# Block products in the linear memory's output projection, and a residual kept off chip

## The chip, the cores and the metric

One core of a Trainium2 chip runs one inference step of a hybrid encoder layer. A core has a matrix engine (TensorE, PE in the profile, with PEld for its weight loads), three engines for elementwise work (VectorE = DVE, ScalarE = ACT, GpSimd = POOL), and SyncE (SP), which here only issues DMAs. Matmuls read operands from the on-chip memory and accumulate in banks of a small second memory (PSUM); DVE and ACT read the banks. The metric is the device time of one execution in microseconds.

## The reference

The layer takes 512 frames of a new stream and 64 of a running one, 576 columns in all, 1024 features wide.

```python
h = layer_norm(ALPHA * x + 0.5 * swiglu_ffn(x, ffn1_w_gu, ffn1_w_down), ln1_g, ln1_b)
z = h @ w_in                       # mLSTM q,k,v,o,i,f | attention q,k,v | gates g_ml, g_att
h_ml  = mlstm(conv(q), conv(k), v, i, f)          # 4 heads of 256, matrix memory, chunks of 64
h_ml  = norm_per_head(h_ml) * ml_norm_g * sigmoid(o)
y_ml  = h_ml @ w_ml_proj                          # 1024 x 1024
y_att = band_attention(...) @ w_att_proj          # 1024 x 1024
merged = sigmoid(g_ml) * y_ml + sigmoid(g_att) * y_att
h = layer_norm(ALPHA * h + merged @ w_out, ln2_g, ln2_b)
y = layer_norm(ALPHA * h + 0.5 * swiglu_ffn(h, ffn2_w_gu, ffn2_w_down), ln3_g, ln3_b)
```

Beside y the step returns the attention's keys and values, the convolution's history and the memory's state. All of it is fp32. The change lies in `y_ml`, `merged` and the residual `ALPHA * h`.

## The kernel before

**Data.** Activations lie transposed: a tile has 128 features in its partitions and 576 columns (time), and 1024 features are eight tiles. A weight tile has 128 partitions and 1024 numbers: the eight 128x128 blocks of one output tile.

**fp32 out of two parts.** A matmul takes rounded operands. Each operand is split into a high part (ACT rounds it) and a low part (the difference, by DVE's tensor_tensor at L150), and each product is three matmuls: high x high, high x low, low x high. For weights in the list `ADDED` the low part is made another way (`add_lo`): ACT writes minus the high part, and a DMA issued by POOL (L197) adds the original to it in place.

**A plain gemm** (`gemm`) computes an output tile as 8 blocks x 3 matmuls in two halves of the columns, 256 and 320: 48 matmuls.

**Block products** (`seven`). Two output tiles j, j+1 and the two halves of the columns (A = 288 to 576, B = 0 to 288) and of the features form a 2x2 block product, which is computed with seven block products instead of eight, in Winograd's form: 7 products x 4 blocks x 3 = 84 matmuls of 288 columns. They need sums of weight blocks and of activation blocks, and sums of results. `seven` takes the weight operands by the names a, u, t, b: a = the first tile's weights, b = half of the second's, u and t = sums (`split_ds`, two raw tiles; t's sums are the last readers of a's raw tile). The order is X from a; Y from a; X += t; Z from u; X += u; Z (or Y) += t; X += b, and after each product `step(n)` runs: ACT copies X after the first and third product, and Z after the fourth, DVE does the rest. X is copied while its bank goes on accumulating, so the next product into X has to wait for the copy. The feed-forward layers and, in four pairs, the attention's projection (`ap_pair`) are computed this way before the change.

**Weights** come through four split buffers (`NWB = 4`) and two raw buffers, in the order of the list `plan`. `pump` loads ahead and splits the next weight when a buffer is free; `done` frees a buffer after its last product.

**Order.** PE's instructions run in the order in which they are written. A small planner (`Order`, `later(dt, fn)`) counts PE time and writes delayed work between the matmuls. The other engines' instructions are ordered by the compiler, by priority (`tc.high_priority(offset=...)`) and readiness; on the chip each engine then works in its fixed order. `issue_after` puts one instruction behind another.

**The stage that changes.** The four heads of the matrix memory run one after the other; a head's last work are transposes (L143) of `hf`, after which two tiles `og` with the head's output are appended to `HF`. Under the last head three gate tiles (60, 61, 62) are computed. After the last head: `gate(7)`, one more gate tile, under which `ht_split` splits the eight tiles HF; then eight plain gemms ("mp", j) with the matmul operand H; each result half is multiplied by its gate on DVE, the attention's part (`matt`, loaded from DRAM tile MD by SP) is added by POOL, and the sum is split into `mg`, the operand of the out projection ("o", j).

**The residual.** The operands H of w_in (the first norm's output in two parts, 16 of the 24 buffers of the pool `slots`) stay on chip until the second norm takes both parts as its residual (two DVE operations per half tile, `Norm.residual`). The second norm's own result goes to DRAM (XD) for the third norm, which loads it again; the `mg` tiles have a pool of their own.

Of the kernel before, what the change touches and what calls it, by code (L numbers as in the profile page):

```python
# [10 lines left out]
F32 = mybir.dt.float32  # L11
# [6 lines left out]
P = 128  # L18
NP_ = 512
NS = 64  # L20
# [66 lines left out]
def tile_layer(ctx: ExitStack, tc: tile.TileContext, ins, outs):  # L87
# [75 lines left out]
    def blank(out, like, behind=None):  # L163
# [15 lines left out]
        | {("ap", j) for j in range(KT)} | {("gu2", 1, 1)}  # L179
# [27 lines left out]
    ds = {}  # L207

    def split_ds(c):
# [8 lines left out]
        def put(a, t):  # L218
            n = t.shape[1]
            ds["hi"] = act(hi[:, a:a + n], t)  # L220
            tt(lo[:, a:a + n], t, f(hi[:, a:a + n]), ALU.subtract)
# [3 lines left out]
        elif what == "u":  # L225
            own = plan[c][0][0] == "dsap" and plan[c][0][1] > 0
            room = lambda: (slot(F32, opool[0], "o") if own else slot(F32))[:, :512]
# [110 lines left out]
    def gemm(tiles, xs, cbs, passes=NORMAL, tags=None):  # L338
# [7 lines left out]
        for p, (tl, hl) in enumerate(passes):  # L346
            nch = len(tiles[tl[0]])
            k0 = 0
            for c in range(nch):
# [4 lines left out]
                for i in range(nk):  # L354
                    k = k0 + i
                    ww = slice(i * P, (i + 1) * P)
                    st, sp = k == 0, c == nch - 1 and i == nk - 1
# [92 lines left out]
    plan += [(("mp", j), ins["w_mp"][j]) for j in range(KT)]  # L450
# [85 lines left out]
    class Norm:  # L536
        def __init__(self, xs, scale, eps, gi, final=None, keep=False, away=None):
            self.away = away
# [37 lines left out]
        def collect(self, j, hf, ps):  # L576
# [11 lines left out]
            else:  # L588
# [6 lines left out]
                if j < KT - 1 and (self.away is None or j + 1 not in DS):  # L595
                    self.residual(j + 1, hf)
# [20 lines left out]
        def shift(self, hf, dh):  # L617
# [3 lines left out]
            dr = self.lp.tile([P, 320], F32R, tag="dr", name=nm("dr"))[:, :n] if self.away is None else \  # L621
# [9 lines left out]
            if self.away is not None and hf == 1:  # L631
# [3 lines left out]
        def moments(self, j, hf, dh):  # L635
# [9 lines left out]
            if j == KT - 1 and self.away is not None:  # L645
                wst["behind"] = last
            if j == KT - 1:
                later(L_JOINT if hf and self.away is not None else L_STATS, lambda: self.stats(hf))
# [8 lines left out]
        def stats(self, hf):  # L657
# [16 lines left out]
            later(J_SPREAD if hf and self.away is not None else L_SPREAD, lambda: self.spread(hf, dg))  # L674
# [61 lines left out]
        def apply(self, j, hf, rb):  # L736
# [9 lines left out]
            if self.final is None:  # L746
# [91 lines left out]
    def seven(name, j, blocks, X, Y, Z, step):  # L838
# [16 lines left out]
        own = name == "dsap"  # L855
# [300 lines left out]
    XD = [away("xd") for _ in range(KT)]  # L1156

    def ffn(xs, n, gi, raw, final=None, prev=None):
        hh = {}
        with tc.tile_pool(name=nm("hr"), bufs=FT, side="right", reuse_waits="tile") as hr, \  # L1160
# [92 lines left out]
            with tc.tile_pool(name=nm("h1"), bufs=n1, side="right", reuse_waits="tile") as h1, \  # L1253
# [4 lines left out]
                          away=[ins["xT"][:, k] for k in range(KT)] if prev is None else XD)  # L1258
# [582 lines left out]
    sgp = gstack.enter_context(tc.tile_pool(name="sg0", bufs=4, side="right", reuse_waits="tile"))  # L1841
# [4 lines left out]
    mp = mstack.enter_context(tc.tile_pool(name="ml", bufs=1, reuse_waits="tile"))  # L1846
# [450 lines left out]
```

## Time and profile before

| | us |
|---|---|
| runs shown: lowest, median, highest of 3 | 1547.39, 1547.59, 1549.40 |
| span of the profiled execution | 1546.8 |
| PE busy | 1531.3 (99%) |
| DVE busy | 1160.4 (75%) |
| ACT busy | 882.5 (57%) |
| POOL busy | 196.6 (13%) |
| last transposes of the last head | 1034.25 |
| eight plain gemms of the linear memory's projection | 1041.74 to 1092.52 |
| second feed-forward layer begins | 1145.17 |

The profile's own execution is told by its span, from the first to the last instruction; what lies around it isn't listed apart. Times are in microseconds from the span's start. In a timeline row stand start, duration, engine, line, operation, output <- inputs, shape and count, and in brackets how long the engine stood before it and what released it; matmuls overlap, so the distance of their starts is what one costs. A row of groups has busy time and mean ns behind the first bar. A windows row has, for each engine, the busy time in that stretch and the count of instructions, then PE's granted clock, DMA's busy share and GB/s. Names such as s, o, H, wh, wl are the program's tiles: wh and wl the high and low part of a weight, wr its raw tile, s a buffer of `slots`, os and H the split operands of the attention's and the linear memory's projection, mg that of the out projection.

### The profile page before, as it was taken

Reading aid. Unit: us, or ns where it says so; the run is one execution under the profiler, and the core shown is the slowest. Engines: PE = TensorE matmul, PEld = TensorE weight load, DVE = VectorE, ACT = ScalarE, POOL = GpSimd, SP = SyncE. Lnnn points to the kernel's source line nnn. Section 1 sums busy time; section 2 is a strip of 40 time slices with the busy share of each in tenths; the row PEclk is TensorE's granted clock in tenths of the full one; section 3 lists DMA queues with packets and bytes.
Section 4 is the critical chain, followed back from the end, with each engine's and each line's share of the span. In section 5 each row is a group of like instructions: output and inputs, shape, how many; then the busy total and the mean of one; then the engine's idle time right before and its main releaser. Section 6 shows DMA issues by size and latency. Waiting matters only on the chain.

```text
span 1546.8 us, 29458 instructions
## 1 busy us (share of the span) xinstructions
PE 1531.3 (99%) x11587; PEld 1516.3 (98%) x11587; DVE 1160.4 (75%) x2186; ACT 882.5 (57%) x1670; POOL 196.6 (13%) x370
## 2 busy tenths in 40 slices
PE   9999999999999999999999999999999999999997
PEld 9999999999999999999999999999999999999997
DVE  7877778756899767887677577775688787787756
ACT  7545446533766557777864877753456454557323
POOL 1000000100200015545200321102120000001000
PEclk9999999999999999999999999999999999999999
DMA  8322223535544449687544965542653223217244
GB/s 246 109 101 91 93 99 102 130 108 146 172 152 143 156 167 239 153 209 169 139 107 147 283 148 133 130 132 82 199 126 104 108 82 110 82 69 190 78 128 150
DMA packets 82228, 213.18 MB, mean 138 GB/s; under 512 B 9513, under 2 KB 23209, under 8 KB 82089
## 3 DMA queue, kind: packets, MB, share of 16 engines
q1 hardware_dynamic: 66088, 172.29, 33.8%
q0 software_dynamic: 14848, 37.30, 13.7%
q8 instruction: 91, 1.49, 0.4%
q10 hardware_dynamic: 1152, 1.70, 0.3%
q14 instruction: 49, 0.39, 0.1%
HBM read 174.82 MB, written 22.22 MB: 127 GB/s over the span
## 4 chain that ended last, share of the span: by engine, by line
PE 84%; DVE 7%; ACT 3%; DMA 3%; issue 2%; POOL 1%; SPq 0%; ACTq 0%; DVEq 0%; POOLq 0%
PE mm L133 69%; PE aux L133 14%; PE aux L143 2%; DVE wl L150 1%; DVE sc L1537 1%; DVE s L150 1%; DVE s L153 1%; ACT wh L147 1%; ACT sc L147 1%; DMA s<-in_xT 1%; DVE o L150 1%; DVE kl L150 1%; DVE sc L157 1%; DMA wr<-in_w_ap 0%; DMA kh<-kh 0%
## 5 line engine op out<-in xcount | busy, mean ns | idle before, releaser
L133 PE MATMUL mm<-s,wh 128*128 128x288 f32 (+2 forms) x3430 | 700.8, 298 | 0.7 <-DVE s L150 0.2
L133 PEld LDWEIGHTS mm<-s,wh 128*128 128x128 f32 x3430 | 548.3, 189 | 3.8 <-DVE s L150 1.6
L133 PE MATMUL mm<-s,wl 128*128 128x288 f32 (+2 forms) x1705 | 503.3, 295 | 0.0
L133 PEld LDWEIGHTS mm<-s,wl 128*128 128x128 f32 x1705 | 321.1, 188 | 0.2 <-DVE wl L150 0.2
L147 ACT ACTIVATE wh<-wr 128x1024 fp32r<-128x1024 f32 (+2 forms) x136 | 133.0, 979 | 141.0 <-PE mm L133 81.7
L133 PE MATMUL mm<-tx,wh 128*128 128x288 f32 x778 | 158.4, 296 | 0.0
L150 DVE TENSOR_TENSOR wl<-wr,wh 128x1024 fp32r<-128x1024 f32 (+2 forms) x97 | 108.9, 1126 | 57.1 <-ACT wh L147 57.0
L133 PEld LDWEIGHTS mm<-tx,wh 128*128 128x128 f32 x778 | 124.9, 188 | 0.0
L133 PE MATMUL mm<-tx,wl 128*128 128x288 f32 x383 | 113.0, 295 | 0.6 <-DVE wl L150 0.6
L925 ACT ACTIVATE wh<-wt 128x1024 fp32r<-128x1024 f32 x53 | 56.2, 1060 | 88.4 <-DVE wt L150 88.4
L150 DVE TENSOR_TENSOR wl<-wt,wh 128x1024 fp32r<-128x1024 f32 x53 | 64.7, 1222 | 52.3 <-ACT wh L925 51.0
L133 PE MATMUL mm<-h,wh 128*128 128x256 f32 (+2 forms) x384 | 78.3, 295 | 0.0
L150 DVE TENSOR_TENSOR wl<-wu,wh 128x1024 fp32r<-128x1024 f32 x50 | 61.2, 1224 | 21.6 <-ACT wh L925 21.6
L197 POOL DMA_DIRECT2D s<-s x16 | 13.7, 854 | 495.0 <-ACT s L147 252.8
L133 PEld LDWEIGHTS mm<-tx,wl 128*128 128x128 f32 x383 | 72.0, 188 | 0.9 <-DVE wl L150 0.9
L147 ACT ACTIVATE h<-h 128x288 f32<-128x288 f32 x80 | 34.9, 437 | 65.2 <-DVE h L150 65.1
L925 ACT ACTIVATE wh<-wu 128x1024 fp32r<-128x1024 f32 x50 | 52.9, 1058 | 32.7 <-PE mm L133 32.5
L150 DVE TENSOR_TENSOR wl<-ws,wh 128x1024 fp32r<-128x1024 f32 x53 | 64.6, 1219 | 0.1
L150 DVE TENSOR_TENSOR ws<-wu 128x1024 f32<-128x1024 f32 x53 | 64.5, 1217 | 0.0
L133 PEld LDWEIGHTS mm<-h,wh 128*128 128x128 f32 x384 | 61.5, 188 | 0.2
L925 ACT ACTIVATE ah<-wu 128x512 fp32r<-128x512 f32 x53 | 33.4, 631 | 44.8 <-PE mm L133 41.3
L133 PE MATMUL mm<-h,wl 128*128 128x256 f32 (+2 forms) x192 | 56.5, 294 | 0.0
(399 smaller groups left out, 3612.6 us busy)
## 6 DMA issues: line engine op xcount, KB each, us to landing
wu<-in_w_gu SPq DMA_DIRECT2D x80, 512.0 KB, 4.3
wr<-in_w_in SPq DMA_DIRECT2D x46, 512.0 KB, 3.7
wr<-in_w_dn SPq DMA_DIRECT2D x40, 512.0 KB, 3.6
wl<-in_w_in POOLq DMA_DIRECT2D x38, 512.0 KB, 6.8
wu<-in_w_in SPq DMA_DIRECT2D x26, 512.0 KB, 4.5
wr<-in_w_dn SPq DMA_DIRECT2D x20, 384.0 KB, 3.7
s<-s POOLq DMA_DIRECT2D x16, 288.0 KB, 3.7
wr<-in_w_ap SPq DMA_DIRECT2D x8, 512.0 KB, 3.6
```

Source lines behind the costliest of these rows:

```text
L133: PE.matmul(out, lhsT, rhs, start=start, stop=stop, **kw)
L143: PE.transpose(out, in_, idn)
L147: return ACT.activation(out, in_, func, **kw)
L150: return (eng or DVE).tensor_tensor(out, a, b, op=op)
L153: return DVE.scalar_tensor_tensor(out=out, in0=a, scalar=s, in1=b, op0=op0, op1=op1)
L157: return (eng or DVE).tensor_scalar(out=out, in0=a, scalar1=s1, scalar2=s2, op0=op0, **kw)
L197: return POOL.dma_start(lo, src, accum_op=ALU.add)
L925: self.last = ACT.activation(hi, src, AF.Copy)
L1537: DVE.tensor_tensor_reduce(out=out, in0=ps, in1=g, op0=ALU.add, op1=ALU.min, scale=-1.0, scalar=3e38, accum_out=acc)
```

## The change

The linear memory's projection keeps its first two output tiles as plain gemms; the other six become three pairs of block products ("dsmp"). For that:

- the rows of w_ml_proj are reordered on the host so that blocks i and 4 + i of the product are HF[2i] and HF[2i+1], and the plain gemms take their blocks in the order 0, 4, 1, 5, ...;
- `whole(i)` splits two tiles of HF as before, and `blocks(i)` makes the sums of halves in place (four half-width DVE operations), rounds two sums and makes two low parts, most of them with `add_lo`. `first_blocks` does this for HF[0] to HF[3] and one block pair under the end of the last head, at low priority; a pool `mq` now holds what the heads no longer need by then and is closed for it;
- the weights a and b of a pair, and the two plain tiles' weights, get their low part by `add_lo` (ACT copy and POOL DMA); the sums u and t have four buffers of their own (`qpool`);
- the attention's part is added for six of eight tiles by an accumulating DMA of POOL from DRAM into the gated tile, which is split 10500 planner units later; the last pair adds two loaded tiles on DVE and splits in parts;
- `mg` lies in `slots`, in buffers that H leaves;
- the first norm's result is written to DRAM (XH, 16 stores on SP), and the second norm loads its residual from there (eight loads on SP, behind the last weight load), one DVE operation per half tile.

```diff
+    qpool = []
...
             ds["hi"] = act(hi[:, a:a + n], t)
+            if plan[c][0][0] == "dsmp" and what in "ab":
+                add_lo(lo[:, :n], hi[:, :n], plan[c][1])
+                return
             tt(lo[:, a:a + n], t, f(hi[:, a:a + n]), ALU.subtract)
...
-    plan += [(("mp", j), ins["w_mp"][j]) for j in range(KT)]
+    plan += [(("mp", j), ins["w_mp"][j]) for j in range(2)]
+    for j in range(2, KT, 2):
+        a, b = ins["w_mp"][j], ins["w_mp"][j + 1]
+        plan += [(("dsmp", j, x), w) for x, w in (("a", a), ("u", b), ("t", None), ("b", b[:, :512]))]
...
                     act(dh, dh, AF.Identity, bias=b_)
-                    if self.away is None:
-                        SP.dma_start(XD[j][:, t0:t0 + n], dh)
+                    SP.dma_start(self.store[j][:, t0:t0 + n], dh)
...
             tt(Wl[:w, :n], d[:w, :n], f(Wh[:w, :n]), ALU.subtract)
+            if h == 3 and b == 4:
+                later(0, first_blocks)
...
+    def whole(i):
+
+        r = HF[2 * i], HF[2 * i + 1]
+        for e in range(2):
+            hi, lo = HT.p[4 * e + i] = slot(F32R, htp[i > 1], "H"), slot(F32R, htp[i > 1], "H")
+            act(hi, r[e])
+            tt(lo, r[e], f(hi), ALU.subtract)
+
+    def blocks(i):
+
+        r2, r1 = HF[2 * i], HF[2 * i + 1]
+        (h2, l2), (h1, l1) = HT.p[i], HT.p[4 + i]
+        hp_, lp_, hm, lm = (slot(F32R, htp[i > 1], "H") for _ in range(4))
+        tt(r1[:, A], r1[:, A], r1[:, B], ALU.subtract)
+        tt(r1[:, B], r2[:, B], r1[:, B], ALU.subtract)
+        stt(r2[:, B], r1[:, A], -1.0, r2[:, B], ALU.mult, ALU.subtract)
+        stt(r2[:, A], r2[:, B], -1.0, r2[:, A], ALU.mult, ALU.subtract)
+        for hi, lo, r in ((hp_, lp_, r2), (hm, lm, r1)):
+            wst["rounded"] = act(hi, r)
+            if i < 2 or r is r1:
+                add_lo(lo, hi, r)
+            else:
+                tt(lo, r, f(hi), ALU.subtract)
...
+    def first_blocks():
+        bstack.close()
+        htp.append(hts.enter_context(tc.tile_pool(name="ht0", bufs=16, side="right", reuse_waits="tile")))
+        with tc.high_priority(offset=-1500):
+            for i in range(2):
+                whole(i)
+            blocks(0)
...
-    od.bg.append((1300, ht_split()))
-    matt = [slot(F32) if j < 4 else slot(F32, gmp, "gm") for j in range(KT)]
-    for m, d in zip(matt, MD):
-        SP.dma_start(m, d)
+    with tc.high_priority(offset=300):
+        for i in range(2, 4):
+            whole(i)
+    for i in range(1, 4):
+        blocks(i)
+    matt = {j: slot(F32) for j in (KT - 2, KT - 1)}
+    for j, m in matt.items():
+        SP.dma_start(m, MD[j])
...
+    def mp_pair(j):
+        X, Y, Z = bank("mm")[:, :HT_], bank("aux")[:, :HT_], bank("mm")[:, :HT_]
...
+            if last:
+                e, cc = {5: (1, B), 6: (0, slice(0, T)), 7: (1, A)}.get(n, (0, None))
+                if cc is not None:
+                    with tc.high_priority(offset=60 if n == 7 else 0):
+                        tt(sg[j + e][:, cc], sg[j + e][:, cc], matt[j + e][:, cc], ALU.add)
+                        split(e, cc)
+            elif n > 5:
+                POOL.dma_start(sg[j + n - 6], MD[j + n - 6], accum_op=ALU.add)
+                later(10500, lambda: split(n - 6))
...
+        seven("dsmp", j, HB, X, Y, Z, step)
...
-    for j in range(KT):
-        gemm(one(("mp", j)), HT, [mp_cb(j)])
+    for j in range(2):
+        gemm(one(("mp", j)), HT, [mp_cb(j)], order=(0, 4, 1, 5, 2, 6, 3, 7))
+    for j in range(2, KT, 2):
+        mp_pair(j)
+    od.drain()
...
-    ln2 = Norm(H, ALPHA, EPS, 1, keep=True)
+    ln2 = Norm(H, ALPHA, EPS, 1, keep=True, away=XH, store=XD)
+    with tc.issue_after(wst["load"].ins):
+        for j in range(KT):
+            ln2.fetch(j, SP)
```

More of the change, by code (lines that the diff above doesn't have):

```diff
@@ L336, in get, with gemm @@
             return self.p[k]
-    def gemm(tiles, xs, cbs, passes=NORMAL, tags=None):
+    def gemm(tiles, xs, cbs, passes=NORMAL, tags=None, order=None):
         ids = {}
@@ L594, in collect @@
                     self.moments(j, hf, dh)
[L595 removed]
+                if j < KT - 1 and not (self.down and j + 1 in DS):
                     self.residual(j + 1, hf)
@@ L630, in shift @@
             self.shifted.add(hf)
-            if self.away is not None and hf == 1:
+            if self.down and hf == 1:
                 for j in range(2, LAST[1]):
```

135 lines of the change are left out of this document (80 added, 55 removed).

## The prediction

> **What bounds the kernel now.** I read the page first, then the waits of PE, then the windows of the stages around the linear memory's projection, then PE's timeline of that projection and of the attention projection, which already runs as block products.
>
> ```profile
> span 1546.8 us, 29458 instructions
> PE 1531.3 (99%) x11587; PEld 1516.3 (98%) x11587; DVE 1160.4 (75%) x2186; ACT 882.5 (57%) x1670; POOL 196.6 (13%) x370
> PE aux L143 <- DVE ptl L150: 2.1, 4, 1.0
> PE mm L133 <- ACT o L147: 0.2, 1, 0.2
> ```
>
> ```profile
> core 0: us, PE busy (x) PEld busy (x) DVE busy (x) ACT busy (x) POOL busy (x), PEclk, DMA share, GB/s
> 790.00:803.00 13.00, 13.00 (x100) 13.00 (x99) 13.00 (x27) 8.36 (x16) 0.00 (x0) 1.00 0.13 42
> 1042.00:1054.00 12.00, 12.00 (x94) 12.00 (x92) 6.81 (x11) 4.27 (x7) 2.35 (x3) 1.00 0.29 87
> 1054.00:1066.00 12.00, 12.00 (x94) 12.00 (x93) 6.45 (x10) 3.90 (x6) 3.23 (x4) 1.00 0.22 77
> 1105.00:1118.00 13.00, 13.00 (x101) 13.00 (x100) 11.25 (x27) 6.42 (x9) 0.84 (x1) 1.00 0.78 187
> ```
>
> PE is busy for 99% of the span, at clock 1.00, and its longest wait is 1.0 us. So only two things move the time: matmul work taken away, and new waits of PE. In the projection (1042 to 1092) DVE is a little over half busy and ACT a third: that is the room into which the change puts its additions.
>
> The profiled execution has a span of 1546.8; the median shown is 1547.59, 0.8 above it. The sum is made on the span, and 0.8 is added at the end. I call a change within 0.2% (3.1 us) no change, about what a measurement of this kernel can tell.
>
> **The change part by part. PE.**
>
> ```profile
> 1041.74 0.40 PE L133 MATMUL mm<-H,wh 128*128 128x256 f32 x2
> 1048.09 0.40 PE L133 MATMUL mm<-H,wh 128*128 128x256 f32 x2
> 803.55 0.43 PE L133 MATMUL mm<-os,wh 128*128 128x288 f32 x2
> 814.67 0.42 PE L133 MATMUL mm<-os,wh 128*128 128x288 f32 x2
> 840.84 0.53 PE L133 MATMUL mm<-os,wh 128*128 128x288 f32 x2 [0.23 <-ACT o L147]
> 849.07 0.40 PE L133 MATMUL mm<-s,wh 128*128 128x256 f32 x2
> ```
>
> A plain tile takes 1048.09 - 1041.74 = 6.35, a pair 12.70 (96 matmuls). The first pair of the attention projection, 84 matmuls of 288 columns, takes 814.67 - 803.55 = 11.12. Three pairs save 3 x 1.58 = 4.74: the most that the change can bring. The attention projection's four pairs took 849.07 - 803.55 = 45.52, 11.38 each, because its third products had to wait (the row at 840.84 is one). At that mean three pairs save 3 x 1.32 = 3.96. I take 3.96, since the new pairs have the same order of products and copies.
>
> [...]
>
> **Operands of the projection.** Before: eight splits of HF, then nothing. After: the same eight, plus 16 half-width sums on DVE, eight roundings on ACT, and eight low parts: two on DVE, six as an ACT copy and an accumulating DMA of POOL.
>
> ```profile
> 1031.97 1.69 DVE L157 TENSOR_SCALAR hf<-hf,mv,mrs 128x256 f32<-128x256 f32 x5
> 1034.25 1.25 PE L143 MATMUL aux<-ident,hf 128*128 128x128 f32 x10
> L150 DVE TENSOR_TENSOR H<-og,H 128x576 fp32r<-128x576 f32 x8 | 5.7, 755 | 0.4 <-ACT H L147 0.3
> L147 ACT ACTIVATE H<-og 128x576 fp32r<-128x576 f32 x8 | 5.0, 675 | 0.0
> L147 ACT ACTIVATE wh<-wr 128x1024 fp32r<-128x1024 f32 x10 | 10.6, 1059 | 15.8 <-PE mm L133 15.8
> 806.98 0.45 DVE L150 TENSOR_TENSOR o<-o,aux 128x288 f32<-128x288 f32 x1 [1.90 <-PE aux L133]
> 817.41 0.69 DVE L150 TENSOR_TENSOR wl<-o,wh 128x512 fp32r<-128x512 f32 x1 [0.23 <-ACT wh L147]
> 828.10 0.63 ACT L147 ACTIVATE wh<-o 128x512 fp32r<-128x512 f32 x1 [3.02 <-DVE o L150]
> 828.63 0.39 ACT L147 ACTIVATE o<-mm 128x288 f32<-128x288 f32 x1
> ```
>
> HF0 to HF3 and the first block sums fit the holes under the last head. What remains must be done between the end of the last transposes (1034.25 + 1.25 = 1035.5) and the first product that takes a block sum, third in its pair, at 1041.74 + 12.70 + 2/7 x 11.12 = 1057.6: 22.1 us. ACT then has 4 splits and 10 block operations (14 x 0.675), four weight passes (4 x 1.06), the half passes of u and t (4 x 0.63) and three gate copies (0.4 each): 17.4. DVE has 4 x 0.755, 12 x 0.45, 2 x 0.755, u and t 8 x 0.69, four gatings and four og products (0.45 each): 19.0. Side by side both fit under the last gate's matmuls and the plain pair; before the attention projection DVE was full for 13 us (first windows row) and PE stayed busy. Cost 0; if that cover fails because the two wait for each other in turn, the price is that of a rival below.
>
> **Weights.** Per pair before: 2 x 1.06 on ACT and two low parts on DVE. After: a and b low parts by ACT copy and POOL DMA, u and t sums on DVE: ACT 2.12 + 4 x 0.63 + 1.26 = 5.9, DVE 8 x 0.69 = 5.5. With evictions (ACT 3 x 0.4, DVE 5 x 0.45 + 0.755) and the splits of two result tiles (ACT 1.35, DVE 1.5) a pair has 8.5 us of ACT and 10.0 of DVE in 11.12. DVE at 90% is what makes waits likely. The rows at 828 show how: ACT stood 3.02 us at a weight rounding that wanted a DVE sum, and the copy of X queued behind it ran at 828.63, so the next product into X started late. The 11.38 contains two such waits.
>
> New against that pattern is the low part of a:
>
> ```profile
> 806.78 1.06 ACT L147 ACTIVATE wh<-wr 128x1024 fp32r<-128x1024 f32 x1 [0.97 <-PE aux L133]
> 980.39 1.06 ACT L147 ACTIVATE wh<-wr 128x1024 fp32r<-128x1024 f32 x1 [0.56 <-PE mm L133]
> 981.72 1.06 ACT L147 ACTIVATE wl<-wh 128x1024 fp32r<-128x1024 f32 x1
> 983.08 0.85 POOL L197 DMA_DIRECT2D wl<-in_w_in  x1 [0.99 <-ACT wl L147]
> L197 POOL DMA_DIRECT2D wl<-in_w_in x18: 844/860/952, 852.3 to 1008.4; - x18
> DMA to landing us min/median/max: 5.3/6.1/11.0
> ```
>
> With four weight buffers the next a can be rounded only when this pair's a is free, 806.78 - 803.55 = 3.23 after the pair's start. From rounding to DMA issue is 983.08 - 980.39 = 2.69, landing 5.3 at best and 6.1 at the median of the 18 in 840 to 1015. That is 11.2 to 12.0 after the start, and PE wants it with the next pair's third matmul, two matmuls of 11.12 / 84 = 0.13 in: at 11.39. Behind the DMA's wait for the copy POOL has only the DMAs that add the attention part, which have a pair's time. So at two pair starts the wait is 0 to 0.6, and ACT's queue can add 0.5. As a late start also gives the third product time, it partly replaces the wait counted in the 11.38. I take 0.1 each, 0.2; ends 0 and 2.2.
>
> ```profile
> 828.77 2.61 SPq L266 DMA_DIRECT2D wr<-in_w_ap  x2
> 832.29 1.06 ACT L147 ACTIVATE wh<-wr 128x1024 fp32r<-128x1024 f32 x1 [0.74 <-DMA wr<-in_w_ap]
> ```
>
> There the next a was even loaded late (its raw buffer waits for the t sums), 832.29 being 6.5 after that pair's start (814.67 + 11.12). With own buffers for the sums the new t sums can run earlier; if not, the last pair's a lands 3 us later. That is in the upper end.
>
> **Around it.** Last pair to out projection: after the sixth product come an eviction, a gating, an addition, a rounding and a low part, 0.45 + 2 x 0.755 + 0.675 + 0.755 = 3.4 and hops; the last product (11.12 / 7 = 1.6) and the six steps before k = 6 (6 x 0.35, from 6.35 by columns) give 3.7. I take 0.2; ends 0 and 1.5, as DVE is busy. hf is ready at 1033.66, 0.59 before the transposes; one low-priority split of 0.755 in front of it costs 0.2, so 0.1 (ends 0 and 0.6). The other parts:
>
> ```profile
> 1098.42 0.28 PE L133 MATMUL aux<-dr,ones_r 128*128 128x256 f32 x1
> s<-xd SPq DMA_DIRECT2D x6, 288.0 KB, 4.9
> s<-s POOLq DMA_DIRECT2D x16, 288.0 KB, 3.7
> 401.48 0.36 SPq L266 DMA_DIRECT2D wr<-in_w_in  x1
> 415.15 0.65 SPq L1687 DMA_DIRECT2D s<-in_vpast  x1
> 1141.22 0.46 PE L133 MATMUL aux<-mg,wh 128*128 128x320 f32 x2
> 1144.35 0.40 ACT L147 ACTIVATE s<-s 128x256 fp32r<-128x256 f32 x1
> 1145.17 0.50 PE L133 MATMUL mm<-s,eh 128*128 128x256 f32 x2
> ```
>
> Adding the attention part by accumulating DMA (3.7 to land) takes 16 POOL additions away and has a pair's time; nothing waits. The residual from memory: eight loads of 288 KB queue on SP behind the out weights. The first, issued about when the out projection starts and landing in 4.9, then passes one DVE and one ACT operation before the mean matmul, which stands 5.9 after that start (1098.42 - 1041.74 - 8 x 6.35): 0, ends 0 and 0.5. It also takes one of two DVE operations of each residual away, 16 x 0.45 = 7 us in a stage where DVE is 11.25 of 13 busy; PE does not wait there, so 0. The 16 new stores after the first norm, about 0.36 us each on SP, should mostly fall into SP's hole from 401.84 to 415.15, with no weight load queued behind them: 0, ends 0 and 0.5. At the second norm the new operands take over buffers of the out projection's input; PE's last pass frees the first two within 0.5 us of 1141.22, two more each 0.44 us, and ACT first writes at 1144.35, so that still fits.
>
> Sum: 1546.8 - 3.96 + 0.2 + 0.2 + 0.1 = 1543.3; with 0.8, 1544.1.
>
> **The rivals.** *Waits eat half.* Pair starts 2.2, third products as before (0.78 for three pairs at the mean), edge 1.0, tail and first residual 0.6: 4.6 of waits, 1546.8 - 4.74 + 4.6 + 0.8 = 1547.5; over a whole band of 1.7 to 7.8 us of waits the time is within 0.2%, middle 1546. For it: DVE at 90%, tight landings. Against: the same structure lost 1.0 in four pairs. 0.30.
>
> *The first block pair starts late: slower.* Place: the 22.1 us computed above. ACT's 17.4 and DVE's 19.0 feed each other, each in its written order; without any overlap they need 36.4, 14.3 too long, and the time is 1546.8 - 4.74 + 14.3 + 0.8 = 1557. For it: ACT's 3.02 us stand at 828.10 is such a wait. Against: the full DVE of 790 to 803. It decides for slower where less than 6.5 us of ACT's work overlaps (a wait of 7.8); 0.12, at about 1552 in the middle.
>
> *The accumulating DMAs land late: slower.* Two pair starts wait L - 5.4 each; at L = 9.5 that is 8.2 and with the edges 0.5 the time is 1551.6. It decides at L = 9.1; the rows reach 11.0, but DMA's share in this stage is only 0.22. 0.08. [...]
>
> **How the numbers follow.** Forecast 0.50, at 1544.1, own range 1542.8 (no wait: 1546.8 - 4.74 + 0.8) to 1544.5 (0.2% below). Rivals 0.30, 0.12, 0.08. Low is 1542.7; high is 1550, which takes in the unchanged band and leaves out most of the 0.20 of slower. Faster 0.50, same 0.30, slower 0.20.
>
> **What would show it.** Right: 36 fewer matmuls; three pairs of 11.1 to 11.8 between the plain pair and the out projection, with waits of PE under 0.7 each; six fewer SP loads of the attention part. Wrong: PE rows named by wl at a pair's start, by the block operands (H) at the first third product, by DVE mg at the out projection, or by hf at the transposes, adding to over 1.7.

## The result

The changed kernel takes 1563.55 us (median of 4 runs, 1559.28 to 1565.28), the kernel before 1548.49 (1547.39 to 1549.63): a ratio of 1.0088, with a 95% interval of 1.0070 to 1.0106. The change is slower by about 0.9%, which by that interval is 11 to 16 us. Forecast were 1544.1 with a range of 1542.7 to 1550.

The profiled execution has a span of 1562.9, 16.1 more than the one of before. From the page of the changed kernel, then three rows of its view of PE's waits (us in total, times, longest):

```profile
span 1562.9 us, 29516 instructions
PE 1534.5 (98%) x11551; PEld 1518.7 (97%) x11551; DVE 1168.6 (75%) x2206; ACT 904.2 (58%) x1706; POOL 201.6 (13%) x374
PE mm L133 <- ACT og L147: 5.9, 2, 3.4
PE mm L133 <- ACT s L147: 4.6, 1, 4.6
PE mm L133 <- DMA wl<-in_w_in: 1.1, 1, 1.1
```

The 36 matmuls are gone, as the change says (11551 against 11587), and PE is nevertheless busy for 3 us longer. None of these three waits is in the kernel before. PE's timeline gives the places: the first matmul of the projection, of its three pairs, of the out projection and of the out projection's third tile, with the stops between them. The kernel before has two rows to set beside them, in the second fence.

```profile
1044.34 0.40 PE L133 MATMUL mm<-H,wh 128*128 128x256 f32 x2
1057.01 0.42 PE L133 MATMUL mm<-H,wh 128*128 128x288 f32 x2
1066.92 0.85 PE L133 MATMUL mm<-H,wh 128*128 128x288 f32 x2 [3.38 <-ACT og L147]
1074.21 0.43 PE L133 MATMUL mm<-H,wh 128*128 128x288 f32 x2
1083.20 0.53 PE L133 MATMUL mm<-H,wh 128*128 128x288 f32 x2 [2.47 <-ACT og L147]
1088.35 0.43 PE L133 MATMUL mm<-H,wh 128*128 128x288 f32 x2
1099.47 0.40 PE L133 MATMUL mm<-s,wh 128*128 128x256 f32 x2
1105.68 0.58 PE L133 MATMUL mm<-s,wh 128*128 128x256 f32 x1 [4.61 <-ACT s L147]
1107.42 0.58 PE L133 MATMUL mm<-s,wh 128*128 128x256 f32 x1 [1.16 <-DVE s L150]
1121.65 0.40 PE L133 MATMUL mm<-s,wh 128*128 128x256 f32 x2
```

```profile
1092.52 0.40 PE L133 MATMUL mm<-mg,wh 128*128 128x256 f32 x2
1105.44 0.39 PE L133 MATMUL mm<-mg,wh 128*128 128x256 f32 x2
```

The third pair takes 1099.47 - 1088.35 = 11.12, exactly what was predicted for a pair without waits. The first takes 17.20 and the second 14.14. Cut at these marks, the 16.1 us fall as follows (the projection is eight tiles; "first two out tiles" runs from the out projection's first matmul to its third tile):

| us | before | after | difference |
|---|---|---|---|
| start to projection | 1041.74 | 1044.34 | +2.60 |
| projection | 50.78 | 55.13 | +4.35 |
| first two out tiles | 12.92 | 22.18 | +9.26 |
| from there to the end | 441.36 | 441.25 | -0.11 |

So nothing is lost behind the out projection's second tile. The 2.60 ahead of the projection are taken apart with the last experiment; the larger part of the loss is at two places: before the fifth product of the first two pairs, and at the fifth operand of the out projection. What PE waited for there was ScalarE (ACT). Its timeline around the first pair:

```profile
1058.80 0.41 ACT L147 ACTIVATE og<-mm 128x288 f32<-128x288 f32 x1
1060.26 1.06 ACT L147 ACTIVATE wh<-wr 128x1024 fp32r<-128x1024 f32 x1 [1.05 <-PE aux L133]
1064.94 0.68 ACT L147 ACTIVATE s<-sg 128x576 fp32r<-128x576 f32 x1 [3.62 <-DMA sg<-md]
1065.53 1.04 ACT L147 ACTIVATE wl<-wh 128x1024 fp32r<-128x1024 f32 x1
1066.47 0.69 ACT L147 ACTIVATE og<-mm 128x288 f32<-128x288 f32 x2
```

The first row copies X behind the first product, in time. The last row is the pair of copies that free X for the fifth product and take Z. X was complete when the third product ended, at 1057.01 + 3 x 11.12 / 7 = 1061.8, and its copy ran 4.7 later. In front of the copies in ACT's queue stands the split of tile 1 (`s<-sg`, with a weight's copy `wl<-wh` behind it), and it stood 3.62 us until the attention part had been added to that tile by the accumulating DMA. The view of the tiles sg, between 1040 and 1112, tells what that cost ACT in sum (us, times) and how long these DMAs took from issue to landing:

```profile
  DMA sg<-md: 10.4, 3
DMA to landing us min/median/max: 5.0/5.9/7.5
```

One of the three, 4.06 us in the second plain tile, cost nothing, because a plain tile has no copy on ACT. The other two are the two waits of PE.

A second loss comes behind the waits. These are windows of the changed kernel:

```profile
1064.00:1068.00 4.00, 1.08 (x4) 1.08 (x5) 2.05 (x3) 2.23 (x4) 0.86 (x1) 0.69 0.16 29
1068.00:1072.00 4.00, 4.00 (x19) 4.00 (x18) 1.74 (x4) 1.15 (x2) 0.00 (x0) 0.50 0.90 187
1080.00:1084.00 4.00, 1.53 (x12) 1.30 (x11) 2.57 (x4) 1.93 (x3) 0.86 (x1) 1.00 0.79 142
1104.00:1108.00 4.00, 1.16 (x3) 0.87 (x4) 4.00 (x5) 2.20 (x4) 0.00 (x0) 0.50 0.89 322
1108.00:1112.00 4.00, 4.00 (x18) 4.00 (x18) 0.45 (x2) 0.42 (x1) 0.00 (x0) 0.50 0.95 324
```

Behind the stop of 3.38 and behind that of 4.61 the granted clock is 0.50: 19 and 18 matmuls in 4 us, against 30 and 32 in the two windows from 1084 to 1092, at clock 1.00. These two follow the 2.47 at 1083, behind which the clock stayed at 1.00.

### The profile page after: what moved, and what is told of

Its sections match the earlier page's. It is cut to its first block, busy times and chain, and to the rows that moved or that the text cites. A ratio compares the mean times of both kernels' runs of the same rounds, so it can differ in the third digit from the quotient of the medians.

```text
span 1562.9 us, 29516 instructions
## 1 busy us (share of the span) xinstructions
PE 1534.5 (98%) x11551; PEld 1518.7 (97%) x11551; DVE 1168.6 (75%) x2206; ACT 904.2 (58%) x1706; POOL 201.6 (13%) x374
## 4 chain that ended last, share of the span: by engine, by line
PE 78%; DVE 9%; issue 4%; DMA 4%; ACT 4%; POOL 1%; SPq 0%; DVEq 0%; ACTq 0%; POOLq 0%
PE mm L133 63%; PE aux L133 13%; PE aux L143 2%; DVE wl L150 1%; DVE s L150 1%; DVE sc L1548 1%; ACT wh L147 1%; DVE s L153 1%; DMA wr<-in_w_in 1%; DVE sc L157 1%; ACT sc L147 1%; DVE o L150 1%; DMA wl<-in_w_in 1%; DVE ptl L150 1%; DVE kl L150 1%
## 5 line engine op out<-in xcount | busy, mean ns | idle before, releaser
L133 PE MATMUL mm<-s,wh 128*128 128x288 f32 (+2 forms) x3654 | 749.6, 299 | 6.7 <-ACT s L147 4.6
L133 PEld LDWEIGHTS mm<-s,wh 128*128 128x128 f32 x3654 | 587.6, 190 | 10.1 <-ACT s L147 4.8
L133 PE MATMUL mm<-s,wl 128*128 128x288 f32 (+2 forms) x1817 | 538.1, 296 | 1.1 <-DMA wl<-in_w_in 1.1
L133 PEld LDWEIGHTS mm<-s,wl 128*128 128x128 f32 x1817 | 344.1, 189 | 1.5 <-DMA wl<-in_w_in 1.3
L150 DVE TENSOR_TENSOR wl<-wr,wh 128x1024 fp32r<-128x1024 f32 (+2 forms) x89 | 96.1, 1084 | 58.0 <-ACT wh L147 57.9
L147 ACT ACTIVATE s<-s 128x576 fp32r<-128x576 f32 (+6 forms) x94 | 49.8, 556 | 14.5 <-DVE s L150 7.7
```

What stands on the lines that cost most here:

```text
L133: PE.matmul(out, lhsT, rhs, start=start, stop=stop, **kw)
L147: return ACT.activation(out, in_, func, **kw)
L150: return (eng or DVE).tensor_tensor(out, a, b, op=op)
```

## The experiments

The theory: the splits of tiles 1 to 3 wait for a DMA at the head of ACT's queue, and the copies that PE needs wait behind them; at the out projection the splits of tiles 4 and 5 are simply too far back in the queue. The rivals: ACT and VectorE (DVE) have too much to do in a pair, wherever the splits stand; or the accumulating DMAs are too late for any place; or the rest of the change costs the time.

Each profile was cut at the marks used above; the columns are us from the start to the projection, the projection, the first two out tiles, and the span. A span is that of one execution, while a ratio takes in 4 to 11 runs of a version: where they differ, the ratio decides. For "plain tiles" and for "both" the profiled execution was the fastest of its runs (1550.47 with a median of 1551.20, and 1547.26 with a median of 1549.48).

| kernel | start to | projection | two out tiles | span | ratio to before, 95% |
|---|---|---|---|---|---|
| before | 1041.74 | 50.78 | 12.92 | 1546.8 | |
| before, again | 1042.23 | 50.78 | 12.92 | 1547.6 | |
| after | 1044.34 | 55.13 | 22.18 | 1562.9 | 1.0088 (1.0070 to 1.0106) |
| after, again | 1043.47 | 55.03 | 21.77 | 1561.5 | |
| splits behind the copies | 1043.21 | 48.21 | 19.17 | 1551.8 | 1.0035 (1.0025 to 1.0045) |
| no attention add | 1042.98 | 46.05 | 20.21 | 1550.5 | 1.0019 (1.0009 to 1.0028) |
| gaps filled | 1045.14 | 52.85 | 20.20 | 1559.4 | 1.0084 (1.0069 to 1.0099) |
| plain tiles, rest of the change | 1042.42 | 50.51 | 14.19 | 1548.8 | 1.0016 (1.0006 to 1.0025) |
| splits behind, adds later | 1043.51 | 47.31 | 19.13 | 1551.1 | 1.0029 (1.0018 to 1.0041) |
| splits behind, edge order | 1044.04 | 47.55 | 16.67 | 1549.5 | 1.0029 (1.0018 to 1.0041) |
| both | 1042.54 | 46.39 | 15.41 | 1545.5 | 1.0005 (0.9997 to 1.0014) |
| both, POOL order | 1045.18 | 47.91 | 15.46 | 1549.9 | 1.0007 (0.9998 to 1.0016) |
| both, five operands ahead | 1044.48 | 46.73 | 17.24 | 1549.6 | 1.0002 (0.9992 to 1.0011) |

**The splits behind the copies.** Against the changed kernel:

```diff
+    def behind(i):
+        s, (hi, lo) = sg[i], mg.p[i]
+        with tc.issue_after(turn["copy"].ins):
+            act(hi, s)
+        with tc.issue_after(turn["evict"].ins):
+            tt(lo, s, f(hi), ALU.subtract)
...
+                if n == 4:
+                    turn["copy"] = cp
...
+                    if n == 5:
+                        turn["evict"] = ev
...
+            if n == 5:
+                for i in pend:
+                    behind(i)
+                pend.clear()
...
                 POOL.dma_start(sg[j + n - 6], MD[j + n - 6], accum_op=ALU.add)
-                later(10500, lambda: split(n - 6))
+                pend.append(j + n - 6)
```

> The six splits that wait for an attention part are put behind the fourth product's copy (ScalarE) and the fifth step's eviction (VectorE) of the next pair; nothing else moves. Theory (they stand at the head of ScalarE's queue and hold up the copies behind them): no wait of over 0.3 before a fifth product, three pairs of 11.1 to 11.5 each, the wait at the out projection under 1, the granted clock 1.00 there; 3.4 + 2.5 + 5.8 of waits and about 5 of half rate go, so the span is about 1546, level with the kernel before within 3 us. Rival (ScalarE and VectorE simply have too much work in a pair): the waits move to other products, pairs of 12 to 14, span 1553 to 1560. Rival (the accumulating DMAs are too late wherever the splits stand): the out projection waits 4 or more for its fifth operand, span 1553 or more.

The ratio fell from 1.0088 to 1.0035. No fifth product waits any more, and the first pair takes 11.23. That much of the theory holds: the same work in another order removes the two waits. But the span is 1551.8, not 1546, because three waits came to light that the larger ones had covered (the second fence is a window behind the second of them):

```profile
1080.45 0.40 PE L133 MATMUL mm<-H,wl 128*128 128x288 f32 x1 [1.29 <-DMA wl<-in_w_mp]
1096.42 0.38 PE L133 MATMUL mm<-s,wh 128*128 128x256 f32 x1 [2.68 <-ACT s L147]
1103.38 0.39 PE L133 MATMUL aux<-dr,ones_r 128*128 128x256 f32 x1 [0.69 <-ACT dr L147]
```

```profile
1098.60:1102.00 3.40, 3.40 (x15) 3.40 (x14) 0.00 (x0) 0.00 (x0) 0.00 (x0) 0.50 0.95 318
```

The first is the low part of `a` at the third pair's start, at its third matmul. The second is now the last pair's own tile 6, no longer tiles 4 and 5; it is longer than the 1 expected, and the clock, expected at 1.00 there, fell to 0.50 behind it. The third is at the first residual.

**Without the attention part.** The six tiles' accumulating DMAs are left out, the splits stay where they are.

```diff
             elif n > 5:
-                POOL.dma_start(sg[j + n - 6], MD[j + n - 6], accum_op=ALU.add)
                 later(10500, lambda: split(n - 6))
...
-                POOL.dma_start(s, MD[j], accum_op=ALU.add)
```

> The six accumulating DMAs of the attention part are left out, so the six merged tiles lack it; the splits stay where the order puts them. Theory (in a pair the splits wait for the DMA, at the out projection for their place in the queue): both waits at the fifth products go with the half rate behind the first, 8 us, but the out projection still waits 3 to 5 for tiles 4 and 5, since their splits stand behind two weight roundings: span 1553 to 1556. Rival (too much work): the fifth products still wait, span over 1558. Rival (the out projection waits for the DMA): that wait goes too, span 1545 to 1548.

The projection takes 46.05 and the three pairs 11.13, 11.13 and 11.12, with as many instructions of ACT and DVE as in the changed kernel: the rival of too much work is out. The price of a pair is right too, since 50.78 - 46.05 = 4.73 against the forecast's most of 4.74. The out projection still waits, with no DMA behind it (PE's timeline of this run, then ACT's):

```profile
1093.70 0.58 PE L133 MATMUL mm<-s,wh 128*128 128x256 f32 x1 [3.08 <-ACT s L147]
1095.44 0.58 PE L133 MATMUL mm<-s,wh 128*128 128x256 f32 x1 [1.16 <-DVE s L150]
```

```profile
1092.04 1.04 ACT L147 ACTIVATE wh<-wr 128x1024 fp32r<-128x1024 f32 x1
1092.98 1.24 ACT L147 ACTIVATE s<-s 128x576 fp32r<-128x576 f32 x2
```

The splits of tiles 4 and 5 (the last row) come after the last pair's own and after an out weight's rounding. So there the place in the queue is the cause, and the rival of a late DMA is out for that wait. The span, 1550.5, is below the 1553 to 1556 expected; the projection began 1.36 earlier than in the first profile of the changed kernel. The low parts of weights, POOL's other DMAs in this stage, landed after 4.7 to 5.3 us here, against 5.1 to 6.6 in the changed kernel.

**The gaps filled with matmuls.** All waits stay; PE has something to do in them.

```diff
+        if name == "dsmp" and j == 2:
+            fill(24)
         product(X, "u", 0, "t3", False, False)
...
+                    if tiles[0][0][0] == ("o", 0) and k == 4 and 0 in hl:
+                        ps = bank()[:, :256]
+                        for _ in range(34):
+                            PE.matmul(ps, parts[ids[0, 0]][0][:, 0:P], xs.p[0][0][:, 0:256], start=True, stop=True)
```

> Every wait stays, but PE is given matmuls into a spare bank, 24 of 288 columns ahead of the first pair's fifth product and 34 of 256 ahead of the fifth operand of the out projection, each a little less than the wait there. Theory (the slow matmuls behind these waits are the granted clock, which fell because PE stood): clock 1.00 after both, the first pair 14.6 to 15.2 instead of 17.2, the out projection's first tile 2.5 to 3 shorter, span 1557 to 1559. Rival (they are slow for another reason, late operands or the transfers): the same half rate, span 1562 to 1564, or longer by the fill.

```profile
1064.00:1068.00 4.00, 3.87 (x29) 3.64 (x28) 1.59 (x3) 2.23 (x4) 0.41 (x1) 1.00 0.28 50
1068.00:1072.00 4.00, 4.00 (x33) 4.00 (x32) 2.85 (x6) 2.17 (x4) 0.45 (x1) 1.00 0.77 127
1108.00:1112.00 4.00, 4.00 (x30) 4.00 (x29) 0.60 (x2) 1.01 (x3) 0.00 (x0) 1.00 0.96 346
```

The clock stays at 1.00 through the windows that showed 0.50 before. The first pair falls from 17.20 to 14.93, within the forecast, and the first two out tiles from 22.18 to 20.20 (less than the 2.5 to 3 expected); the span is 1559.4, just above the 1557 to 1559 expected. So some 4.3 us of the loss are the clock and not the wait itself. In the span 0.8 of that is hidden by a later start of the projection, and the runs' ratio, 1.0084, is too wide in its interval to show it; the stages show it.

**Plain tiles with the rest of the change.** No block operands and no pairs; normed input off chip, accumulating DMAs for tiles 0 to 5, order of k and buffers as in the changed kernel.

```diff
-    for j in range(2):
+    for j in range(KT):
         gemm(one(("mp", j)), HT, [mp_cb(j)], order=(0, 4, 1, 5, 2, 6, 3, 7))
-    for j in range(2, KT, 2):
-        mp_pair(j)
...
+                if j in matt:
+                    tt(s, s, matt[j], ALU.add)
+                else:
+                    POOL.dma_start(s, MD[j], accum_op=ALU.add)
```

> All eight tiles of the projection plain, without block operands, with the rest of the change (normed input off chip, accumulating DMAs for tiles 0 to 5, order of k, buffers). Theory (the loss is the pairs' waits, and before the projection the rest costs 2.3 to 2.6): the projection's eight tiles take 50.8, the out projection waits under 1, span 1548.5 to 1550. Rival (the rest is what costs): a span of 1555 or more. Rival (the rest costs nothing, and the 2.6 came by chance): 1546 to 1547.5.

The span is 1548.8, as expected, and the ratio 1.0016 (1.0006 to 1.0025), which is 1 to 4 us. The rest of the change has a price of its own, 1.27 of it in the first two out tiles, and the pairs must first earn that. But ahead of the projection it lost 0.68 and not 2.3 to 2.6.

This run is also a control for the theory. Its splits wait for the accumulating DMAs on ACT as well, the first five for 4.1 to 6.8 us each, as in this row:

```profile
1073.61 0.69 ACT L147 ACTIVATE s<-sg 128x576 fp32r<-128x576 f32 x1 [4.74 <-DMA sg<-md]
```

Yet the projection takes 50.51, against 50.78 before the change. In this run the waiting splits cost the projection nothing: no copy that PE needs stands behind them.

**Later attention adds, and another order at the edge.** Two repairs on top of the splits behind the copies, first one at a time. The DMAs for tiles 2 and 3 go behind the next pair's low part on POOL:

```diff
+                if n == 4 and held:
+                    with tc.issue_after(wst["low"].ins):
+                        for i in held:
+                            POOL.dma_start(sg[i], MD[i], accum_op=ALU.add)
```

> Splits as in the run with the splits behind, and the two accumulating DMAs of tiles 2 and 3 issued behind that of the next pair's a low part instead of ahead of it; their splits move to the second step of the last pair. Theory (in that run the third pair's start waited 1.3 for a's low part, and the second pair's last product 0.2 for b's, because two transfers of 288 KB stood ahead of them in POOL's queue): both waits go, three pairs of 11.1 to 11.4, span 1549.5 to 1550.5. Rival (the low part lands 7.6 after its issue because of the other traffic, the loads among it): the wait at the pair's start stays above 1, span 1551 to 1552.

The waits for low parts are gone and their slowest landing between 1050 and 1090 fell, in the view of the tiles wl, from the first of these rows (splits behind) to the second (adds later); the third fence is the timeline with adds later:

```profile
DMA to landing us min/median/max: 5.6/6.3/8.1
```

```profile
DMA to landing us min/median/max: 4.8/5.4/6.8
```

```profile
1082.88 0.69 ACT L147 ACTIVATE s<-sg 128x576 fp32r<-128x576 f32 x1 [2.24 <-DMA sg<-md]
1085.49 0.69 ACT L147 ACTIVATE og<-mm 128x288 f32<-128x288 f32 x2
1085.94 0.54 PE L133 MATMUL mm<-H,wh 128*128 128x288 f32 x2 [0.98 <-ACT og L147]
```

But the splits, now in the last pair ahead of its copies, stand there for their DMA, and the last pair's fifth product waits 0.98. It is the first theory's mechanism again, made by my own edit. The projection still went from 48.21 to 47.31. The span, 1551.1, missed its range, but some 1.5 of it has nothing to do with the edit: in this execution the clock fell far ahead of the projection, in the attention, behind a stop of 1.00 that the kernel before has too (its PE row `ptl`, at 629.28), where the clock was 1.00 from 630 to 638.

```profile
630.90:634.30 3.40, 3.40 (x16) 3.40 (x16) 1.16 (x7) 1.80 (x7) 1.28 (x4) 0.50 0.63 136
```

The other repair gives the out projection's first tile six operands of both halves before the last two:

```diff
+    for ks in (range(6), range(6, KT)):
+        for hf in range(2):
+            for k in ks:
```

> Splits as in the run with the splits behind, and the out projection's first tile takes operands 0 to 5 of both halves before operands 6 and 7 of either. Theory (the 2.7 and 0.4 of waits there are cover that is missing: the last pair's chain ends late and only six steps stood before it; and the clock falls behind them): six more steps of 0.44 cover 2.6, waits of under 0.8 remain, the clock is 1.00, span 1546.5 to 1548. Rival (the first residual, whose first half now ends 2.6 later, gives it back at the norm): span 1550 or more.

The wait for tile 6 went (2.68 to 0), the first two out tiles from 19.17 to 16.67, and the clock stayed at 1.00. But the rival had a point:

```profile
1100.90 1.06 ACT L147 ACTIVATE wh<-wr 128x1024 fp32r<-128x1024 f32 x1 [4.37 <-DMA wr<-in_w_o]
1103.71 0.39 PE L133 MATMUL aux<-dr,ones_r 128*128 128x256 f32 x1 [1.72 <-ACT dr L147]
```

The first residual's copy on ACT (`dr`) stands behind a weight rounding that waits 4.37 for its load. Span 1549.5, not 1546.5 to 1548. The two repairs together, with the last pair's additions and splits at higher priority:

```diff
-                    with tc.high_priority(offset=60 if n == 7 else 0):
+                    with tc.high_priority(offset=60):
```

> Both of the two edits above, and the last pair's attention additions and splits at the priority of its evictions. Theory (the pairs are worth what their matmuls are, once nothing waits; the rest of the change costs the 2 of the run with plain tiles): the pairs save 4.7, span 1544.5 to 1546.5, ratio to the kernel before 0.998 to 1.000. Rival (the additions only change place and other waits come): ratio above 1.001.

The span of 1545.5 lies inside the expectation, but by luck: this execution was the fastest of 11, 2.2 below their median. The ratio, 1.0005 (0.9997 to 1.0014), lies between theory and rival. The projection is down to 46.39; the first two out tiles keep 2.49 more than before. Two more attempts at what was left, each on top of that. First POOL's order before the linear memory's first head:

```diff
+    def blanks():
+        with tc.issue_after(wst["pooled"].ins):
+            POOL.memset(hf_[NS:P, 4, :], 0.0)
...
+    later(9000, blanks)
```

> As the run with both, and the set-up memory fills before the linear memory's first head issued behind the weights' accumulating DMAs on POOL, where the kernel before has them. Theory (the wait for wl in the first head, 0.4 to 1.1 in every run with the change and none in the kernel before, is these fills ahead of the DMA): that wait goes, 0.4 to 1.1 less than the run with both, ratio to the kernel before 0.997 to 0.999. Rival (the DMA is late because its weights arrive later): the wait stays, same time.

The wait for wl in the first head went, and the low parts there (the view of the tiles wl from 850 to 866) landed as in the second of these rows; the first is the changed kernel's:

```profile
DMA to landing us min/median/max: 9.4/11.2/11.3
```

```profile
DMA to landing us min/median/max: 8.2/8.4/9.6
```

This one profile does not show that the fills were the cause: in the run with the edge order the wait is absent as well, with the fills where the change has them. The ratio did not move (1.0007), as other waits came: 0.52 for `vl` a little later, and 1.16 for a low part at the second pair's start. Then the order at the edge:

```diff
-    for ks in (range(6), range(6, KT)):
+    for ks in (range(5), range(5, KT)):
```

> As the run with both edits, but the out projection's first tile takes operands 0 to 4 of both halves ahead of 5 to 7. Theory (in the run with both, 1.1 of wait was left there, for the low part of tile 5, which came 1.1 after the sixth operand step of the first half): the wait goes or stays under 0.4, 0.8 to 1.1 less than the run with both, ratio to the kernel before 0.9985 to 1.0005; with that the change's three pairs are no more than level with what the rest of it costs. Rival (the wait moves to operand 6): same time as the run with both, ratio 1.000 to 1.0015.

The wait for tile 5 went, but the timeline has another, and two windows show the clock, over the stop and behind it:

```profile
1101.85 1.06 ACT L147 ACTIVATE wh<-wr 128x1024 fp32r<-128x1024 f32 x1 [2.33 <-DMA wr<-in_w_o]
1103.59 0.42 PE L133 MATMUL aux<-dr,ones_r 128*128 128x320 f32 x1 [2.12 <-ACT dr L147]
```

```profile
1101.60:1105.00 3.40, 1.41 (x9) 1.41 (x10) 2.06 (x4) 2.59 (x6) 0.00 (x0) 1.00 1.03 389
1105.00:1108.40 3.40, 3.40 (x15) 3.40 (x14) 1.98 (x6) 1.39 (x4) 0.00 (x0) 0.50 0.94 365
```

Again the residual's copy stands behind a weight rounding that waits for its load (2.33), PE waits 2.12, and behind that the clock falls to 0.50; the first two out tiles took 17.24, longer than with six operands ahead. Ratio 1.0002 (0.9992 to 1.0011). No version here beats the kernel before; the repaired ones cannot be told from it.

**Both kernels profiled once more**, unchanged:

> The kernel before, unchanged, profiled once more. In its first profile the linear memory's projection began at 1041.74; with the change it began between 1042.4 and 1045.2 in ten profiles. Theory (about 1 of that is the change, the two waits named by dg and by wl, and the rest differs from one execution to the next): it begins between 1042 and 1044 here, with no wait named by dg or by wl from w_in in the first head. Rival (all of it is the change): 1041.5 to 1042 again.

> The changed kernel, unchanged, profiled once more. Theory: the same waits at the two fifth products and at the out projection (3 to 4, 2 to 3, 4 to 6 in all) with half the granted clock behind the first and the last, the projection 54 to 56 long, the out projection's first two tiles 21.5 to 22.5; the projection's start differs by up to 2 from the first profile. Rival (the waits were those of one execution): they differ by more than 1.5.

The changed kernel waited 3.83 and 2.37 (and 0.49) in the pairs and 5.16 and 1.16 at the out projection, a little over the 6 expected: the waits belong to the order, not to one execution. The projection began at 1043.47 in it, and at 1042.23 in the kernel before, without a wait named dg or wl in the first head. Over all profiles it began at 1041.7 and 1042.2 without the change and between 1042.4 and 1045.2 with it.

Cut at matmuls that both kernels have, this spread falls into parts. Up to the first norm, at 402, the eleven profiles with the change lie between 1.05 earlier and 0.93 later than the first one of the kernel before, which has most likely nothing to do with the change: the other one of that kernel lies 0.34 later. At the first norm, where PE's wait is named dg (0.23 to 0.52), all eleven lose 0.65 to 0.95, and the second of the kernel before loses nothing. The rows show the place, from SP before, then SP and ACT after:

```profile
395.57 0.82 SPq L917 DMA_DIRECT2D wu<-in_w_in  x2
```

```profile
397.19 0.32 SPq L764 DMA_DIRECT2D xh<-s  x1
398.01 0.83 SPq L928 DMA_DIRECT2D wu<-in_w_in  x2
401.52 1.06 ACT L147 ACTIVATE wh<-wu 128x1024 fp32r<-128x1024 f32 x1 [2.09 <-DMA wu<-in_w_in]
```

Stores of the normed input (`xh`) now stand ahead of a weight's load in SP's queue, so the load is issued later; ACT waits for it at the weight's rounding (2.09, and 1.37 before), and right behind that rounding stands the small copy `m` from which dg is made. It is the same mechanism as in the pairs, at a third place; no run took the stores out to test it. The wait for wl in the first head costs 0 to 1.4 and comes and goes. The last transposes take 0.3 longer in every version with pairs and not in the one with plain tiles. In the first profile of the changed kernel these parts are 0.4, 0.7, 1.35 and 0.3, and the remaining -0.2 are small differences between them; so about 1.0 of its 2.60 is in every profile with the pairs.

## Why the prediction was wrong

**The step that failed** is this one: "Adding the attention part by accumulating DMA (3.7 to land) takes 16 POOL additions away and has a pair's time; nothing waits." The tile does have a pair's time until the out projection needs it. But the instruction that reads it next, the split, stands in ACT's queue well before that, and what is behind it in that queue has no pair's time: the copies that free X. It was priced by who needs the result, not by what stands behind the waiting instruction. The 3.7 was also the landing of another stage; here the DMAs took 5.0 to 7.5. The prediction had shown the mechanism itself, in the rows at 828 of the kernel before, where a weight rounding stood and held up the copy of X, and asked of the weights alone whether it would happen again.

Its cost, by the marks: 3.38 and 2.47 of waits in the pairs and 2.27 of half clock behind the first; the remaining 0.96 of the projection's excess over 46.05 was not separated. Of the 19.6 us between the sum's span of 1543.3 and the 1562.9 measured, 8.1 lie in the projection, 9.1 at the edge and 2.5 ahead of the projection.

**The edge** was the second error: 0.2 with ends 0 and 1.5, measured 9.26, of it 5.77 of waits and some 2 of clock. The prediction followed only the last pair's chain (which alone left 2.7 and 2.8 of wait once the other splits had moved, above its end) and not the splits of tiles 4 and 5, which the order puts behind the last pair's own and behind out-weight roundings.

**The clock** was in no term and no rival: some 4.3 us, as the run with filled gaps shows (2.27 in the first pair and 1.98 in the first two out tiles). The range was made from waits alone and had no room for it.

**Right**: a pair without waits is 11.12 to 11.13, and three of them save 4.73. The operands are ready in the 22.1 us: the first pair's third product waits for nothing, so the rival of the late first pair is refuted. The pair starts, 0.2 with ends 0 and 2.2, were 0 in the changed kernel and 0 to 1.3 in the others, within the ends. The second norm's operands still fit: from the third out tile on the time is the same within 0.11.

**Half right**: the last transposes (0.1 taken, ends 0 and 0.6) take 1.59 instead of 1.25 us, because DVE makes a sum of 0.69 for a weight (`q<-wr,wr`) ahead of `hf`; the place is the predicted one, the work in front another. The first residual from memory (0, ends 0 and 0.5) does not wait in the changed kernel, but did for 0.7 to 2.1 in five of the six versions with the splits behind the copies, in four of them behind a weight rounding on ACT and not for the residual's own landing.

**Wrong besides**: the stores of the normed input were to "fall into SP's hole from 401.84 to 415.15, with no weight load queued behind them" (0, ends 0 and 0.5). Eight of the 16 are issued from 386 to 397, ahead of that hole and with a weight load behind them, and the first norm loses 0.65 to 0.95. The wait for wl in the first head (up to 1.1) was not thought of. Two readings were off without weight in the sum: the longest wait of PE before is 1.1 and not 1.0 (`PE aux L504 <- POOL one L487`), and the middle of the band of the rival in which waits eat half is 1547.6 and not 1546.

Of the rivals, "The accumulating DMAs land late" came nearest, since it is accumulating DMAs that were waited for, but it priced the weights' low parts at PE and not the attention parts at ACT. The low parts of weights landed after at most 6.6 us in the changed kernel and after at most 5.3 without the attention parts, with the same 2206 instructions of DVE in both; the L of 9.1 at which this rival decides for slower was reached in neither. The rival in which waits eat half had 4.6 of them; the pairs and the edge alone had 11.6. The predicted signs of error (wl at a pair's start, H at the third product, hf at the transposes, DVE mg at the edge) name only the last of the places where PE waited, and there the long wait was for ACT (4.61) and only the second for DVE (1.16); a row of ACT waiting for sg was not among them.

## What to carry to other kernels

For every instruction that a change makes wait for a DMA, ask first what stands behind it in its own engine's queue, and how soon PE needs that; when the waiting instruction's own result is due does not bound the cost. Such a split held PE up in no pair behind the copies that PE needs, and cost nothing in a stage that has no such copies (waits of 4.1 to 6.8 on ACT with plain tiles), and a large part of the DMA's landing time ahead of them (3.4 and 2.5 of 5.0 to 7.5). A transformation that saves 5 us of matmuls in 1547 can be lost to one such place, and repairing it here only showed the next wait: at best the kernels were level.

## What the runs showed of the hardware

In these runs a stop of PE could cost more than its length. Behind stops of 3.38 to 5.16 us (both profiles of the changed kernel) the granted clock was 0.50 to 0.80 in the next windows of 4 us, each time; behind 1.72 (edge order), 2.37 and 2.47 (the changed kernel) it stayed at 1.00. In between it was not a matter of one length: it fell to 0.50 behind 2.12 (five operands ahead), behind 2.68 with 0.4 shortly after (splits behind the copies), behind 2.81 with 0.21 shortly after (adds later), and once behind 1.00 (adds later, at 628). The windows of the run with five operands ahead show that the fall can come late: the stop ended at 1103.59, the clock was 1.00 up to 1105.0 and then 0.50 for 3.4 us. What decides whether and when it falls was not shown.

In the projection the low parts of weights landed later where accumulating DMAs of attention parts were on POOL's queue too: after at most 5.3 us without attention parts, after at most 6.6 in the changed kernel, and the one with two attention parts directly ahead of it after 8.1 (splits behind the copies); with these two moved behind it, the same low part landed after 4.8 (adds later). Whether they wait in the queue or share the transfer rate was not separated.
